# The context's modulation moved from the opening loop into the first eight projections

## The chip, the core and the metric

The kernel runs on one core of a Trainium2 chip. Its time is device time in microseconds (us); several runs of a kernel are summed up by their median. The core has five engines with a queue of instructions each: TensorE (PE, matrix products), VectorE (DVE), ScalarE (ACT), GpSimd (POOL) and SyncE (SP, which here only issues transfers). The transfers (DMA) between HBM and the core's memory are done by 16 DMA engines, whichever queue issues them. An instruction on a queue that waits holds up what stands behind it on the same queue.

## The reference, cut to what matters

One layer of a diffusion backbone works on a latent sequence `x` of 1024 tokens and on a context `ctx` of 256 tokens, both 1024 wide. Both are first modulated: scaled and shifted per channel, with vectors that a product of SiLU(c), or SiLU(c_ctx) for the context, with `w_ada` gives. The modulated tensors go through one wide input projection.

```
silu_c, silu_cc = silu(c), silu(c_ctx)
sh_m, sc_m, g_m, sh_f, sc_f, g_f = split(silu_c @ w_ada + b_ada, 6)
csh_m, csc_m, ...                = split(silu_cc @ w_ada + b_ada, 6)
h  = x   * (1 + sc_m)  + sh_m        # latent, 1024 x 1024
hc = ctx * (1 + csc_m) + csh_m       # context, 256 x 1024
gates, q, k, v, p_rwkv, p_sgu       = split(h  @ w_in)
_, _, k_c, v_c, p_rwkv_c, _         = split(hc @ w_in)   # what is used of them
```

Behind that come neighbourhood attention, an RWKV scan in both directions, a gated MLP over chunks (its input is `p_sgu`), the merging of the three, and a feed-forward part. The output is the latent stream alone. All is in float32.

## The kernel before, in words

Everything is laid out with channels on the 128 partitions, and a matrix of 1024 channels is 8 slices (k = 0 to 7). To keep the precision of float32 on PE, each factor is split into a high part (rounded to PE's format) and a low part (the rest), and a product is three matmuls: high x high, high x low, low x high (lines 306 to 308 in the opening loop, 220 to 222 in `mm` for the other projections). The high part is made by ACT, the low part by a subtraction on DVE or POOL.

`phase0a` is the first stage. It makes the modulated inputs and does 31 of the input projections, each of 128 output channels: a weight tile of 128 x 1024 is loaded by SP, split (ACT line 208; in this stage DVE line 212) and multiplied with the slices of the latent (two halves of 512 tokens, 48 matmuls) and, where the projection needs it, of the context (24 matmuls of 256 tokens).

The **opening loop** goes over k. For each k it

- loads two tiles of `w_ada`, 128 x 1024 each (scale and shift of the 128 channels of slice k), into a ring `w5` of 6 buffers;
- makes four rows, i.e. reductions along 1024 elements by DVE with `ada_row` (line 240): scale and shift for the latent (`cb[0]`, SiLU of c) and for the context (`cb[1]`). The latent's rows write their product to a tile `junk`, since the context's rows still need the weights. The results are columns of a small tile `mod`;
- loads the input slices `x` (128 x 1024) and `xc` (128 x 256), two buffers each;
- makes by ACT the high part `hh` (line 284) and, in place, the modulated `x` (line 285), and by POOL the low part `hl` (line 286); and likewise `ch` and `cl` for the context;
- for k below 4 loads and splits the weights of one of the projections 36 to 39 (`FIRST`; POOL line 237 makes the low part), which need the latent alone;
- adds slice k to the sums of the projections begun so far, which stay in eight banks of PSUM. The projection that begins at step k catches up on the slices before.

The opening's PE work is so 6, 18, 30, 42 and then four times 24 matmuls of 512 columns.

Behind the loop the low-rank weights of the decay are loaded and split (`lora_weights`, in a pool that takes the place of the opening's), then the constants of the gate, then the projections run in the order of the list `ms`: 36 to 39 (done already, only evacuated by ACT at line 444, shifted by DVE at lines 447 to 453, and stored from POOL's queue at line 455), 48 and 49 (inputs of the low-rank parts, with context), then for j = 0 to 3 the projections 40+j (RWKV k), 28+j (attention k), 44+j and 32+j, all with context, and among the first two j the four projections 55 to 58 of the gated MLP, which need the latent alone; last 51 to 54 and 50. Work that hangs on a projection (norms at lines 460 and 466, `lora`, transposes at 378 and 380) is put on a list `late` and issued up to three pieces per projection. From the seventh projection on, two more tiles of `w_ada` per projection are loaded into a ring `wa` of two buffers and reduced by DVE, 32 rows in all, for the later parts of the layer.

Who goes first on each engine isn't written by hand: a planner orders the instructions of each engine once, when the program is built, by the order in which the code names them and by its own reckoning of when their inputs are ready. So work can stand a little ahead of its place in the code.

Of the kernel before, what the change touches and what calls it, by code (L numbers as in the profile page):

```python
# [6 lines left out]
F32 = mybir.dt.float32  # L7
F32R = mybir.dt.float32r
BF16 = mybir.dt.bfloat16
AF = mybir.ActivationFunctionType  # L10
ALU = mybir.AluOpType
# [4 lines left out]
P = 128  # L16
D = 1024
S = 1024
CT = 256
# [12 lines left out]
FIRST = (36, 37, 38, 39)  # L32
LATE = 3
NWA, NW5, NT2 = 2, 6, 8
# [22 lines left out]
class Kern:  # L57
# [93 lines left out]
    def constants(self):  # L151
# [21 lines left out]
        self.ada = self.cp.tile([P, 48], F32, name="ada")  # L173

# [68 lines left out]
    def phase0a(self):  # L243
# [21 lines left out]
        for k in range(KT):  # L265
            x = self.bp.tile([P, S], F32, name="x", tag="x", bufs=2)
            xc = self.bp.tile([P, CT], F32, name="xc", tag="xc", bufs=2)
            m = self.cp.tile([P, 4], F32, name=f"mod{k}")
            w = [self.w5()[:, 0:D] for _ in range(2)]
            for i in range(2):  # L270
                nc.sync.dma_start(w[i], a["wada"][8 - 8 * i + k])
            for q in range(2):
                for i, b in enumerate((c["bsc"], bada)):
                    junk = w[i] if q else self.bp.tile([P, D], F32, name="junk", tag="junk", bufs=1)
                    self.ada_row(w[i], q, b[:, k:k + 1], m[:, 2 * i + q:2 * i + q + 1], junk)
            nc.sync.dma_start(x, a["xT"][k])
            nc.sync.dma_start(xc, a["cT"][k])
            hh = hp.tile([P, S], F32R, name=f"hh{k}")
            hl = hp.tile([P, S], F32R, name=f"hl{k}")
            ch = tp.tile([P, CT], F32R, name=f"ch{k}")  # L280
            cl = tp.tile([P, CT], F32R, name=f"cl{k}")
            for (xi, hi, lo, q, n) in ((x, hh, hl, 0, S), (xc, ch, cl, 1, CT)):
                sc_, sh_ = m[:, q:q + 1], m[:, 2 + q:3 + q]
                nc.scalar.activation(hi, xi, AF.Identity, scale=sc_, bias=sh_)
                nc.scalar.activation(xi, xi, AF.Identity, scale=sc_, bias=sh_)
                nc.gpsimd.tensor_tensor(lo, xi, hi.bitcast(F32), ALU.subtract)
            self.h.append((hh, hl))
            self.hc.append((ch, cl))
# [10 lines left out]
            for i, (z, (wh, wl, pss)) in enumerate(first.items()):  # L299
                for k2 in range(0 if i == k else k, k + 1):  # L300
                    q = slice(P * k2, P * k2 + P)
                    hh, hl = self.h[k2]
                    xs = (self.hc[k2], (hh[:, 0:512], hl[:, 0:512]), (hh[:, 512:S], hl[:, 512:S]))
                    for p, (xh, xl) in zip(pss, xs[3 - len(pss):]):
                        p = p[:, 0:xh.shape[1]]
                        nc.tensor.matmul(p, wh[:, q], xh, start=(k2 == 0), stop=False)
                        nc.tensor.matmul(p, wh[:, q], xl, start=False, stop=False)
                        nc.tensor.matmul(p, wl[:, q], xh, start=False, stop=(k2 == KT - 1))
        self.first = {z: w[2] for z, w in first.items()}
        self.cm_b.__exit__(None, None, None)  # L310
        self.cm_b, self.bp = self.pool("lora", side="right")
        self.lora_weights()
# [10 lines left out]
        ms = list(FIRST) + [48, 49]  # L323
        for j in range(4):
            ms += [40 + j, 28 + j] + [55 + 2 * j] * (j < 2) + [44 + j, 32 + j] + [56 + 2 * j] * (j < 2) + [51, 52] * (j == 3)
        ms += [53, 54, 50]
        na = 16
        self.late = []
        for i, m in enumerate(ms):
            late, self.late = self.late[:LATE], self.late[LATE:]  # L330
            (self.proj_gelu if m > 50 else self.proj_rwkv if m >= 36 else self.proj_kv)(m)
            self.run_late(late)
            for _ in range(2):
                if i >= 6 and na < 48:
# [5 lines left out]
        self.ada_rest()  # L340

# [1109 lines left out]
```

## Time and profile before

| | |
|---|---|
| median of 3 runs | 2454.48 us (2444.21 to 2455.71) |
| the profiled execution | 2457.49 us, its span 2455.7 us |
| opening loop's last matmul begins | 83.5 us |
| granted PE clock, mean | 0.973 |
| PE busy in the span | 2350.8 us of 2455.7 |
| HBM read and written | 248.85 MB and 85.99 MB, 136 GB/s over the span |

A line of a timeline shows the start, the duration, engine, source line and operation, then output `<-` inputs by the program's names, shapes, the count, and in brackets the idle time ahead of it and what ended that. A line of a group has the count, then busy time in us and the mean of one in ns, then the idle time ahead of its instructions. A line of the waits has the waiting engine, tile and line, whom it waited for, the sum in us, how many times and the longest. Matmuls overlap on PE, so the spacing of their starts is what counts, not the duration of one.

### The profile page before, as it was taken

How to read it: one execution, taken by the hardware profiler on the slowest of the kernel's cores; microseconds unless marked ns; L12 is line 12 of the kernel's file. 1: busy time of each engine (PE TensorE's matmuls, PEld its weight loads, DVE VectorE, ACT ScalarE, POOL GpSimd, SP SyncE). 2: the span in 40 equal slices, each digit the busy share in tenths (PEclk: the TensorE clock that was granted, in tenths of full speed). 3: DMA queues.
4: the chain of work that ended last, by engine and by line, in shares of the span. 5: the costliest groups of instructions: out<-in, count | busy, mean ns of one | idle time of the engine just before them, and what ended most of it. 6: DMA issues, size and time to landing. Idle time of an engine off the chain costs nothing.

```text
span 2455.7 us, 39343 instructions
## 1 busy us (share of the span) xinstructions
PE 2350.8 (96%) x14520; PEld 1850.5 (75%) x14520; DVE 1606.1 (65%) x3498; ACT 914.9 (37%) x1845; POOL 681.1 (28%) x714
## 2 busy tenths in 40 slices
PE   6999999999999999999999999999889999999997
PEld 4778888776777776677777778778678888887886
DVE  8884446347786778778358873778575555555835
ACT  4443334232343443344345552233433333333321
POOL 6221213441211111211121131142434333425402
PEclk9999999999897999999999999999889999999999
DMA  7675434553342343433277547655223222237551
GB/s 252 208 236 166 140 125 155 167 165 87 98 100 70 100 104 100 104 93 73 66 195 196 173 149 267 192 175 172 78 82 98 78 78 78 86 131 273 166 167 52
DMA packets 276116, 337.44 MB, mean 137 GB/s; under 512 B 123314, under 2 KB 194226, under 8 KB 275924
## 3 DMA queue, kind: packets, MB, share of 16 engines
q1 hardware_dynamic: 208804, 240.91, 33.1%
q10 hardware_dynamic: 54608, 51.40, 6.9%
q0 software_dynamic: 12512, 42.62, 4.7%
q8 instruction: 115, 1.88, 0.3%
q14 instruction: 77, 0.63, 0.1%
HBM read 248.85 MB, written 85.99 MB: 136 GB/s over the span
## 4 chain that ended last, share of the span: by engine, by line
PE 64%; DVE 8%; DMA 4%; issue 3%; ACT 2%; POOL 1%; SPq 0%; DVEq 0%; ACTq 0%; POOLq 0%
PE d L221 10%; PE d L222 10%; PE d L220 10%; PE d L1012 3%; PE pv L896 3%; PE d L1013 3%; PE d L1011 3%; PE ho L731 2%; PE gr L656 2%; PE sc L748 2%; PE pt L882 2%; PE sc L743 1%; PE sc L756 1%; PE gr L655 1%; PE sc L754 1%
## 5 line engine op out<-in xcount | busy, mean ns | idle before, releaser
L221 PE MATMUL d<-hl,wh 128*128 128x512 f32 x1056 | 435.8, 413 | 0.0
L222 PE MATMUL d<-hh,wl 128*128 128x512 f32 x1056 | 434.8, 412 | 0.0
L220 PE MATMUL d<-hh,wh 128*128 128x512 f32 x1056 | 433.8, 411 | 0.0
L221 PEld LDWEIGHTS d<-hl,wh 128*128 128x128 f32 x1056 | 202.1, 191 | 42.4 <-issue 0.7
L222 PEld LDWEIGHTS d<-hh,wl 128*128 128x128 f32 x1056 | 202.1, 191 | 42.3 <-issue 2.0
L220 PEld LDWEIGHTS d<-hh,wh 128*128 128x128 f32 x1056 | 201.9, 191 | 41.2 <-issue 1.6
L212 DVE TENSOR_TENSOR wl<-wr,wh 128x1024 fp32r<-128x1024 f32 x51 | 64.9, 1273 | 159.0 <-ACT wh L208 110.6
L208 ACT ACTIVATE wh<-wr 128x1024 fp32r<-128x1024 f32 x79 | 83.6, 1058 | 194.9 <-PE d L221 160.4
L212 POOL TENSOR_TENSOR wl<-wr,wh 128x256 fp32r<-128x256 f32 x112 | 85.6, 795 | 251.1 <-ACT wh L208 197.1
L237 DVE TENSOR_TENSOR o<-wr,o 128x1024 fp32r<-128x1024 f32 (+1 forms) x64 | 93.5, 1463 | 21.4 <-ACT o L234 21.0
L1012 PE MATMUL d<-dl,ah 128*128 128x512 f32 x252 | 98.7, 392 | 2.2 <-DVE dl L237 2.2
L768 ACT ACTIVATE rv<-sc,E 64x64 f32<-64x64 f32 x152 | 46.5, 308 | 143.2 <-DVE rv L767 131.9
L1011 PE MATMUL d<-dh,ah 128*128 128x512 f32 x252 | 98.8, 392 | 0.0
L1013 PE MATMUL d<-dh,al 128*128 128x512 f32 x252 | 98.7, 392 | 0.0
L234 ACT ACTIVATE o<-wr 128x1024 fp32r<-128x1024 f32 (+1 forms) x64 | 59.2, 926 | 104.0 <-PE d L221 73.1
L896 PE MATMUL pv<-pT,V 128*64 128x128 f32 (+2 forms) x640 | 92.1, 284 | 0.0
L237 DVE TENSOR_TENSOR al<-ar,ah 128x512 fp32r<-128x512 f32 x42 | 40.6, 981 | 78.3 <-ACT ah L234 78.3
L1006 POOL TENSOR_TENSOR wl<-wr,wh 128x1024 fp32r<-128x1024 f32 x16 | 42.6, 2661 | 169.0 <-ACT wh L1005 125.5
L734 DVE TENSOR_TENSOR X<-ho,Dt 48x192 f32<-48x192 f32 (+2 forms) x240 | 68.3, 285 | 24.3 <-PE ho L731 19.6
L1239 POOL TENSOR_TENSOR act<-act 128x512 f32<-128x512 f32 x22 | 28.8, 1309 | 193.9 <-issue 160.2
L896 PEld LDWEIGHTS pv<-pT,V 128*64 128x64 f32 (+2 forms) x640 | 69.1, 138 | 16.4 <-issue 10.8
L767 DVE TENSOR_SCALAR rv<-sc,E 64x64 f32<-64x64 f32 x152 | 41.8, 275 | 56.0 <-PE sc L756 38.9
(402 smaller groups left out, 6123.0 us busy)
## 6 DMA issues: line engine op xcount, KB each, us to landing
wr<-wgu SPq DMA_DIRECT2D x45, 512.0 KB
dr<-wdn SPq DMA_DIRECT2D x42, 512.0 KB
wa<-wada SPq DMA_DIRECT2D x32, 512.0 KB
wr<-win SPq DMA_DIRECT2D x31, 512.0 KB
wr<-win ACTq DMA_DIRECT2D x28, 512.0 KB
s_gt<-stg ACTq DMA_DIRECT2D x48, 256.0 KB
wr<-wbr SPq DMA_DIRECT2D x24, 512.0 KB
g<-s_gt SPq DMA_DIRECT2D x48, 256.0 KB
```

The source lines that it names most:

```text
L208: nc.scalar.activation(hi[:, :n], raw[:, :n], AF.Copy)
L212: (lo_eng or self.lo_eng).tensor_tensor(lo[:, q], raw[:, q], hi[:, q].bitcast(F32), ALU.subtract)
L220: nc.tensor.matmul(ps, w, xh, start=first and k == 0, stop=False)
L221: nc.tensor.matmul(ps, w, xl, start=False, stop=False)
L222: self.last = nc.tensor.matmul(ps, lo[:, P * k:P * k + P], xh, start=False, stop=last and k == n - 1)
L234: nc.scalar.activation(hi, src, AF.Copy)
L237: (lo_eng or nc.vector).tensor_tensor(lo, src, hi.bitcast(F32), ALU.subtract)
L734: nc.vector.tensor_tensor(X[z:z + n, :, t0:64], e[z:z + n], Dt[z:z + n, :, t0:64], ALU.add)
L896: nc.tensor.matmul(o, V[0:k, vt, 64 * e:64 * e + 64], pt[0:k, i, :], start=(i == 0), stop=(i == len(cols) - 1))
L1011: nc.tensor.matmul(ps, xh, wh, start=first, stop=False)
L1012: nc.tensor.matmul(ps, xh, wl, start=False, stop=False)
L1013: nc.tensor.matmul(ps, xl, wh, start=False, stop=last)
```

## The change

A new method `modulated(k, q)` makes slice k of the latent (q = 0) or of the context (q = 1). The opening loop calls it for the latent only: two rows on DVE instead of four, no `xc`, `ch` or `cl`; the rows write their products in place, without `junk`. The context's slice k is made behind projection number k of the list, for the first eight. Its two tiles of `w_ada` are loaded a second time, into the ring `wa` of two buffers. The order of the projections changes, so that the first eight need no context: 36 to 39, then 55 to 58, and then 48 and 49; the four aren't spread among the first two j any more. `lora_weights`, with the change of pools, comes behind the eighth projection. The 32 later rows begin at the tenth projection instead of the seventh.

```diff
         for k in range(KT):
-            x = self.bp.tile([P, S], F32, name="x", tag="x", bufs=2)
-            xc = self.bp.tile([P, CT], F32, name="xc", tag="xc", bufs=2)
-            m = self.cp.tile([P, 4], F32, name=f"mod{k}")
-            w = [self.w5()[:, 0:D] for _ in range(2)]
-            for i in range(2):
-                nc.sync.dma_start(w[i], a["wada"][8 - 8 * i + k])
-            for q in range(2):
-                for i, b in enumerate((c["bsc"], bada)):
-                    junk = w[i] if q else self.bp.tile([P, D], F32, name="junk", tag="junk", bufs=1)
-                    self.ada_row(w[i], q, b[:, k:k + 1], m[:, 2 * i + q:2 * i + q + 1], junk)
...
+            self.modulated(k, 0)
             if k < 4:
                 z = FIRST[k]
...
         self.first = {z: w[2] for z, w in first.items()}
-        self.cm_b.__exit__(None, None, None)
-        self.cm_b, self.bp = self.pool("lora", side="right")
-        self.lora_weights()
...
-        ms = list(FIRST) + [48, 49]
+        ms = list(FIRST) + [55, 56, 57, 58, 48, 49]
         for j in range(4):
-            ms += [40 + j, 28 + j] + [55 + 2 * j] * (j < 2) + [44 + j, 32 + j] + [56 + 2 * j] * (j < 2) + [51, 52] * (j == 3)
+            ms += [40 + j, 28 + j, 44 + j, 32 + j] + [51, 52] * (j == 3)
         ms += [53, 54, 50]
...
             self.run_late(late)
+            if i < 8:
+                self.modulated(i, 1)
+            if i == 7:
+                self.cm_b.__exit__(None, None, None)
+                self.cm_b, self.bp = self.pool("lora", side="right")
+                self.lora_weights()
             for _ in range(2):
-                if i >= 6 and na < 48:
+                if i >= 9 and na < 48:
...
+    def modulated(self, k, q):
+        nc, a, c, v = self.nc, self.a, self.c, self.v
+        n = (S, CT)[q]
+        x = self.bp.tile([P, n], F32, name=f"x{q}", tag=f"x{q}", bufs=2)
+        m = self.mod[:, 16 * q + 2 * k:16 * q + 2 * k + 2]
+        w = [self.tp.tile([P, D], F32, name="wa", tag="wa", bufs=NWA) if q else self.w5()[:, 0:D] for _ in range(2)]
+        for i, b in enumerate((c["bsc"], v("bada"))):
+            nc.sync.dma_start(w[i], a["wada"][8 - 8 * i + k])
+            self.ada_row(w[i], q, b[:, k:k + 1], m[:, i:i + 1], w[i])
+        nc.sync.dma_start(x, a["cT" if q else "xT"][k])
+        p = self.tp if q else self.hp
+        hi, lo = (p.tile([P, n], F32R, name=f"h{z}{q}_{k}") for z in "hl")
+        nc.scalar.activation(hi, x, AF.Identity, scale=m[:, 0:1], bias=m[:, 1:2])
+        nc.scalar.activation(x, x, AF.Identity, scale=m[:, 0:1], bias=m[:, 1:2])
+        nc.gpsimd.tensor_tensor(lo, x, hi.bitcast(F32), ALU.subtract)
+        (self.hc if q else self.h).append((hi, lo))
```

More of the change, by code (lines that the diff above doesn't have):

```diff
@@ L173, in constants @@
         self.ada = self.cp.tile([P, 48], F32, name="ada")
+        self.mod = self.cp.tile([P, 32], F32, name="mod")
     def scratch(self):
@@ L265, in phase0a @@
         for k in range(KT):
-            x = self.bp.tile([P, S], F32, name="x", tag="x", bufs=2)
-            xc = self.bp.tile([P, CT], F32, name="xc", tag="xc", bufs=2)
-            m = self.cp.tile([P, 4], F32, name=f"mod{k}")
-            w = [self.w5()[:, 0:D] for _ in range(2)]
-            for i in range(2):
-                nc.sync.dma_start(w[i], a["wada"][8 - 8 * i + k])
-            for q in range(2):
-                for i, b in enumerate((c["bsc"], bada)):
-                    junk = w[i] if q else self.bp.tile([P, D], F32, name="junk", tag="junk", bufs=1)
-                    self.ada_row(w[i], q, b[:, k:k + 1], m[:, 2 * i + q:2 * i + q + 1], junk)
[L276 to L288, printed above, removed]
+            self.modulated(k, 0)
             if k < 4:
@@ L302, in phase0a @@
                     hh, hl = self.h[k2]
-                    xs = (self.hc[k2], (hh[:, 0:512], hl[:, 0:512]), (hh[:, 512:S], hl[:, 512:S]))
-                    for p, (xh, xl) in zip(pss, xs[3 - len(pss):]):
-                        p = p[:, 0:xh.shape[1]]
+                    xs = ((hh[:, 0:512], hl[:, 0:512]), (hh[:, 512:S], hl[:, 512:S]))
+                    for p, (xh, xl) in zip(pss, xs):
                         nc.tensor.matmul(p, wh[:, q], xh, start=(k2 == 0), stop=False)
```

## The prediction, on record before the run

> **What bounds the kernel now.** I read the page of the profile first: TensorE (PE) is busy nearly the whole span, so a change gains only where PE stands still, or where what it works on could be there sooner.
>
> ```profile
> span 2455.7 us, 39343 instructions
> ...
> PE 2350.8 (96%) x14520; PEld 1850.5 (75%) x14520; DVE 1606.1 (65%) x3498; ACT 914.9 (37%) x1845; POOL 681.1 (28%) x714
> ```
>
> The change touches the projection stage, so the second view is the busy time by stretches there (columns: busy time and count of PE, PEld, DVE, ACT, POOL, then granted clock, DMA share, GB/s).
>
> ```profile
> 15.00:36.00 21.00, 12.17 (x28) 7.28 (x28) 20.82 (x19) 9.30 (x11) 17.29 (x7) 1.00 0.69 243
> 36.00:84.00 48.00, 40.62 (x167) 31.84 (x168) 41.77 (x42) 23.37 (x28) 29.10 (x15) 0.96 0.68 227
> 84.00:140.00 56.00, 54.29 (x279) 45.04 (x279) 52.87 (x67) 18.32 (x25) 3.76 (x7) 1.00 0.65 189
> 140.00:160.00 20.00, 15.66 (x59) 11.75 (x58) 9.69 (x13) 9.63 (x13) 0.00 (x0) 0.83 0.74 228
> 160.00:300.00 140.00, 139.90 (x708) 116.83 (x707) 81.87 (x109) 48.89 (x81) 38.76 (x51) 1.00 0.57 177
> ```
>
> PE idles in the opening loop (up to 84 us), a little around 140 to 160, and hardly anywhere else: 139.90 of 140 us behind that. Third, the waits of PE up to 520 us, which name who ended those gaps:
>
> ```profile
> PE d L307 <- POOL hl L286: 11.0, 7, 3.6
> ...
> PE gr L466 <- DVE w L460: 4.3, 1, 4.3
> ...
> PE d L222 <- DVE wl L212: 1.7, 1, 1.7
> ```
>
> In the opening PE waits for POOL's low halves, `hl`. Why POOL is late shows in the groups of instructions of the first 84 us, and in the timelines of DVE and POOL over one step k:
>
> ```profile
> L286 POOL TENSOR_TENSOR hl<-x,hh 128x1024 fp32r<-128x1024 f32 x8 | 22.2, 2771 | 28.4 <-ACT x L285 28.4
> L240 DVE CUSTOM_DVE_ANT_0 w<-w,cb,der 128x1024 f32<-128x1024 f32 x8 | 20.2, 2528 | 0.2
> L240 DVE CUSTOM_DVE_ANT_0 junk<-w,cb,c_pv 128x1024 f32<-128x1024 f32 x8 | 20.1, 2506 | 0.0
> ...
> L240 DVE CUSTOM_DVE_ANT_0 w<-w,cb,c_pv 128x1024 f32<-128x1024 f32 x8 | 13.3, 1666 | 0.2
> L286 POOL TENSOR_TENSOR cl<-xc,ch 128x256 fp32r<-128x256 f32 x8 | 12.8, 1599 | 0.0
> L240 DVE CUSTOM_DVE_ANT_0 junk<-w,cb,der 128x1024 f32<-128x1024 f32 x8 | 12.7, 1592 | 5.2 <-DMA w<-wada 5.2
> ...
> L237 POOL TENSOR_TENSOR w<-wr,w 128x1024 fp32r<-128x1024 f32 x2 | 6.7, 3370 | 0.0
> L237 POOL TENSOR_TENSOR wl<-wr,wh 128x1024 fp32r<-128x1024 f32 x2 | 6.7, 3337 | 0.0
> ```
> ```profile
> 8.25 1.28 DVE L240 CUSTOM_DVE_ANT_0 junk<-w,cb,der 128x1024 f32<-128x1024 f32 x1 [4.85 <-DMA w<-wada]
> ...
> 42.30 1.28 DVE L240 CUSTOM_DVE_ANT_0 junk<-w,cb,der 128x1024 f32<-128x1024 f32 x1
> 43.51 0.08 DVE L240 DVE_READ_ACCUMULATOR2_ANT mod<- 128x1 f32 x1
> 43.63 3.28 DVE L240 CUSTOM_DVE_ANT_0 w<-w,cb,der 128x1024 f32<-128x1024 f32 x1
> 46.84 0.08 DVE L240 DVE_READ_ACCUMULATOR2_ANT mod<- 128x1 f32 x1
> 46.84 3.41 DVE L240 CUSTOM_DVE_ANT_0 junk<-w,cb,c_pv 128x1024 f32<-128x1024 f32 x1
> ```
> ```profile
> 43.40 2.43 POOL L286 TENSOR_TENSOR hl<-x,hh 128x1024 fp32r<-128x1024 f32 x1 [2.10 <-ACT x L285]
> 45.78 3.38 POOL L237 TENSOR_TENSOR w<-wr,w 128x1024 fp32r<-128x1024 f32 x1
> 49.13 1.72 POOL L286 TENSOR_TENSOR cl<-xc,ch 128x256 fp32r<-128x256 f32 x1
> ...
> 78.22 0.75 POOL L286 TENSOR_TENSOR cl<-xc,ch 128x256 fp32r<-128x256 f32 x1
> ```
>
> The same DVE row takes 1.28 us at 42.30 and 3.28 us at 43.63, while POOL's `hl` runs. The times fit one rule: the two take turns. POOL starts when DVE's row ends (43.58) and holds until 45.78, 2.2 us; the DVE row that was issued at 43.63 then needs 1.1 us and ends at 46.91; POOL's next, issued at 45.78, ends at 49.16, 2.25 us after that. So the price of a DVE row is 1.21 us (42.30 to 43.51), of a wide POOL subtraction 2.25 us and of a narrow one about 0.6 us. The sum over the opening: 32 rows x 1.21 = 38.7, 12 wide subtractions (8 `hl`, 4 weight halves) x 2.25 = 27.0, 8 narrow ones x 0.6 = 4.8, together 70.5 us. From the first row at 8.25 that is 78.8 us; the last POOL instruction ends at 78.97. The opening is bound by DVE and POOL in turn, to within 0.2 us, not by DMA (227 to 243 GB/s) and not by PE.
>
> **The opening after the change.** Half of the rows (16) and all 8 narrow subtractions leave. Left are 16 x 1.21 + 27.0 = 46.4 us of turns, which from 8.25 could be done at 54.7 us. Now PE's own work decides.
>
> ```profile
> 64.27 0.80 PE L307 MATMUL d<-hl,wh 128*128 128x512 f32 x1 [3.07 <-POOL hl L286]
> 64.86 0.63 PE L308 MATMUL d<-hh,wl 128*128 128x512 f32 x1
> 65.28 0.63 PE L306 MATMUL d<-hh,wh 128*128 128x512 f32 x1
> ...
> 66.99 0.48 PE L307 MATMUL d<-hl,wh 128*128 128x512 f32 x1
> ...
> 70.96 0.39 PE L306 MATMUL d<-hh,wh 128*128 128x512 f32 x1
> ...
> 76.42 0.40 PE L306 MATMUL d<-hh,wh 128*128 128x512 f32 x1
> ...
> 83.70 0.28 PE L220 MATMUL d<-ch,wh 128*128 128x256 f32 x1
> ```
>
> From 70.96 to 76.42 PE does the 24 matmuls of one step: 0.2275 us each. The opening has 6, 18, 30, 42 and four times 24 of them, 192 in all. Once `hl` of step 2 is there, 168 are left at most, 38.2 us. When is it there? By turns: seven rows (8.5) and five wide subtractions (11.2) from 8.25 give 28.0; two microseconds more for ACT, which makes `hh` and scales `x` between a row and its subtraction, give 30. PE ends at 30 + 38.2 = 68.2, say 68.5, against 83.7: 15.2 us gained. Steps 3 to 7 do not hold it: their turns are over by about 58 us, behind which only the last 24 matmuls (5.5 us) must follow. Bounds: 66 us, were ACT hidden, and 74.5 us, if step 2 comes no earlier than now:
>
> ```profile
> 32.92 3.36 POOL L286 TENSOR_TENSOR hl<-x,hh 128x1024 fp32r<-128x1024 f32 x1
> ```
>
> (36.3 + 38.2). So the gain lies between 9.2 and 17.7 us. SyncE's queue runs in order, and `x` of step k waits there for `hl` of step k-2 with the next weights behind it; in my count this holds a row back by at most the microseconds already allowed.
>
> **The moved work.** The eight `wada` pairs are read a second time (16 x 512 KB), 16 rows go to DVE, 16 narrow passes to ACT, where they stand among the evacuations, and the 8 narrow subtractions to POOL, whose queue also issues the stores of `r` (line 455) and so may make them wait for a shift. They have the time until projection 48, the first that uses context. Ahead of it PE has the four projections 55 to 58, which are moved forward: 4 x 48 x 0.2275 = 43.7 us, so it comes to 48 at about 68.5 + 43.7 + 2 = 114 us. The rows go through a ring of two buffers; what such a row costs then is shown by the later ones of the same ring:
>
> ```profile
> L240 DVE CUSTOM_DVE_ANT_0 wa<-wa,cb,c_pv 128x1024 f32<-128x1024 f32 x20 | 25.5, 1281 | 11.8 <-DMA wa<-wada 11.7
> ```
>
> These 20 lie between 97.0 and 164.5 us: 3.4 us each, with the waits for their loads. The new ones can begin when the opening's last loads are issued, about 53 us by the count above. 53 + 16 x 3.4 + 3 for ACT and POOL = 110 us: in time with 4 us to spare. I set this at nothing. The cover is PE's 43.7 us on the four latent projections; where it ends, each 0.1 us more per row costs PE 1.6 us (the rival below). It can't bring a gain, since 48 has nothing to do earlier. The low-rank weights, now read behind the rows, are needed only after 49: hidden too. The stage's loads and stores between 53 and 114 us, by their sizes (8.4 MB for `wada`, 3.1 MB for six weights, 1 MB each for context and low-rank weights, 0.8 MB for the gate's constants, 3.1 MB stored), are 17.4 MB, an estimated 285 GB/s, against 189 and 228 in the stretches shown.
>
> **The hand-over at the loop's end.** Here is a new wait. DVE makes the low weight half of the next projection, and works in order:
>
> ```profile
> 80.42 0.75 DVE L447 TENSOR_SCALAR w<-w,der 128x1024 f32<-128x1024 f32 x1 [5.88 <-ACT w L444]
> ...
> 85.46 1.22 DVE L212 TENSOR_TENSOR wl<-wr,wh 128x1024 fp32r<-128x1024 f32 x1
> ...
> 86.73 0.38 PE L222 MATMUL d<-ch,wl 128*128 128x256 f32 x1 [1.71 <-DVE wl L212]
> ```
>
> Five shift instructions stand ahead of it (80.42 to 85.46), and PE waits 1.71 us. After the change, context rows are also queued there; one to three of them, 1.2 to 3.6 us, come on top, and without the context's matmuls PE has less to do meanwhile. Everything on PE is queued behind that matmul, and ACT's evacuations and the shifts of the next projections behind PE. I take 2 us more (0 to 5). The gap at 64.27 shows that a stop of 3.07 us also costs the clock: up to 66.99 the matmuls go at 0.43 us, seven of them 0.2 us late each, 1.4 us. The Trainium skill (page TensorE: Matmul & The Clock Gate, section Why this matters for your kernels) warns of idle gaps over about 3 us between bursts of matmuls; the trace agrees, and by that rule a hand-over of 3.7 us would make the sum 1.4 us worse.
>
> **The gap at 147.** The wait of 4.3 us for L460 (a granted clock of 0.83 in that stretch) costs, with the slow restart priced at 64.27, 5.7 us. L460 stands on DVE among the rows of the other shifts and gates, which begin at the tenth projection now instead of the seventh; but the projection that needs L460, 40, comes at the eleventh instead of the seventh. I keep it at no change (between 5.7 gained and a second such gap, 5.7 lost). The rest of the stage has the same matmuls; with 55 to 58 no longer spread between projections whose DVE work is heavy, DVE has fewer pauses, for which I bound 0 to 3 us and take 0.
>
> **Sum.** -15.2 + 2 = -13.2 us. The profiled execution took 2457.49 us with a span of 2455.7, 3 us above the median of the runs; 2457.5 - 13.2 = 2444.3 there, and 2454.5 - 13.2 = 2441.3 against the median. PE is on the path almost without a break behind the stage, so what is gained here is kept.
>
> **Rivals.** *The gap at 147 goes too*: 13.2 + 5.7 = 18.9, giving 2435.6. For it: it hangs on one row and its load. Against: rows and loads are as dense as before. *DVE's queue eats the gain*: hand-over at its worst (5), the pauses (3) and another late weight half, some 10 us in all, giving about 2451. For it: between 53 and 114 us DVE gets 16 rows (16 x 1.28 = 20), twelve shift instructions (5.04 us for five, so 12), and seven halves of weights (7 x 1.22 = 9), 41 of 61 us, in an order fixed beforehand. Against: between 84 and 140 us it is busy for 52.87 of 56, and PE for 54.29, the 1.71 of the hand-over being all that is missing. *The opening is held by loads*: SyncE's order, with each step's `x` behind an `hl` and the weights behind `x`, brings step 2 no sooner than now: 9.2 - 2 = 7 us gained, 2447. Against: the `hl` that `x` waits for come sooner themselves. *Slower*: the ring of two buffers becomes the bound. Rows may take (114 - 53 - 3) / 16 = 3.6 us each; each 0.1 above costs 1.6 us at the start of 48. At 4.4 us the gain is gone, at one and a half times today's 3.4, 5.1 us, PE loses 24 us and the kernel takes 2465. For it: the 285 GB/s, and that rows that wait hold the weight halves behind them. Against: idle DVE before 66 us lets the first rows run at once. That the context isn't moved at all can't be: the loop simply no longer makes it.
>
> **Chances.** Forecast (9 to 17 gained) 0.50; the gap goes too 0.14; DVE's queue 0.17; loads 0.07; slower 0.12. A measurement of this kernel tells about 0.5%, 12.3 us, from no change. The forecast lies on that line: 0.30 of its 0.50 is above. Faster: 0.30 + 0.14 = 0.44. Slower by over 0.5%: 0.09 of the last case. Same: 0.47. The range goes from 2433 (the gap gone and 2 us more) to 2454 (nothing gained); some 0.12 lies above it and 0.05 below. The likeliest case's own range is 2437 to 2446.
>
> **What would show it.** Right: 16 rows and no `cl` ahead of about 55 us; `hl` waits of PE down from 11 us to under 5, all in the first 30 us; first matmul of projection 55 near 68.5; 192 matmuls without a gap from step 2; the context's rows at L240 over by 110. Wrong: the first matmul of 55 after 75; a wait of PE for a `ch` or `cl` at 48; waits for `wl` of 56 to 58; a PE wait for L460 longer than 4.3.

## The result, and the profile after

The changed kernel takes 2472.14 us in the median of 6 runs (2463.14 to 2477.46), beside 2455.1 for the kernel before on the same chip: a ratio of 1.0074, with a 95% interval of 1.0044 to 1.0103. It is slower by 0.7%, and it lies above the range that was forecast (2433 to 2454). The profiled execution has a span of 2472.1 us, 16.4 more than before.

The page, whose first lines answer to those of before:

```profile
span 2472.1 us, 39365 instructions
...
PE 2358.0 (95%) x14520; PEld 1846.0 (75%) x14520; DVE 1603.1 (65%) x3498; ACT 909.8 (37%) x1840; POOL 677.1 (27%) x714
```

PE has as many instructions as before and is busy 7.2 us longer. That is the first sign that not only waits came in.

The opening went as forecast. The groups of instructions of its first 69 us, and PE around its end (lines have moved: DVE's rows are now in L241, `hl` in L337, the projections' three matmuls in L221 to L223, `wl` in L213):

```profile
L337 POOL TENSOR_TENSOR hl<-x,hh 128x1024 fp32r<-128x1024 f32 (+1 forms) x9 | 23.6, 2619 | 24.1 <-ACT x L336 24.1
L241 DVE CUSTOM_DVE_ANT_0 w<-w,cb,c_pv 128x1024 f32<-128x1024 f32 x8 | 22.9, 2859 | 0.0
L241 DVE CUSTOM_DVE_ANT_0 w<-w,cb,der 128x1024 f32<-128x1024 f32 x8 | 17.6, 2196 | 11.2 <-DMA w<-wada 11.2
```
```profile
68.99 0.39 PE L286 MATMUL gr<-hh,w 128*128 128x512 f32 x1
69.21 0.40 PE L221 MATMUL d<-hh,wh 128*128 128x512 f32 x1
```

Sixteen rows on DVE instead of 32, and the next projection's first matmul at 69.21 instead of 83.70: 14.5 us gained, where 15.2 were forecast. The stretches and the waits of PE behind it:

```profile
36.00:69.00 33.00, 33.00 (x145) 26.87 (x145) 23.35 (x21) 14.18 (x15) 15.83 (x7) 1.00 0.74 249
69.00:90.00 21.00, 14.88 (x62) 10.56 (x60) 21.00 (x28) 9.93 (x15) 4.48 (x6) 0.91 0.72 243
90.00:101.00 11.00, 8.81 (x30) 7.02 (x31) 7.24 (x11) 2.40 (x4) 1.75 (x3) 0.71 0.91 312
101.00:155.00 54.00, 54.00 (x273) 44.95 (x272) 25.19 (x36) 17.53 (x28) 4.75 (x6) 1.00 0.89 238
155.00:195.00 40.00, 30.27 (x146) 25.35 (x145) 36.52 (x60) 11.89 (x14) 8.43 (x12) 0.91 0.62 216
195.00:260.00 65.00, 56.39 (x277) 45.98 (x276) 51.33 (x76) 22.35 (x35) 24.23 (x30) 0.95 0.75 237
260.00:400.00 140.00, 139.83 (x725) 116.46 (x725) 78.31 (x90) 51.17 (x85) 34.83 (x50) 1.00 0.40 133
```
```profile
PE d L223 <- DVE wl L213: 18.0, 3, 8.7
PE gr L376 <- ACT t L378: 6.0, 1, 6.0
...
PE d L285 <- POOL hl L337: 1.7, 1, 1.7
```

PE is unbroken from 36 to 69 us, and the wait for `hl` fell from 11.0 to 1.7. Then come three holes, in 69 to 90, 155 to 195 and 195 to 260. In the first DVE is busy for 21.00 of 21 us while PE waits for DVE's `wl`; in each, the granted clock also falls.

The second loss is in no view of waits. The gate-up part of the feed-forward, which the change doesn't touch, by the first and last start of 22 products on POOL in it, first before, then after:

```profile
L1239 POOL TENSOR_TENSOR act<-act x22: 1288/1300/1599, 1801.2 to 2193.9; 128x512 f32<-128x512 f32 x22
```
```profile
L1237 POOL TENSOR_TENSOR act<-act x22: 1275/1287/1594, 1811.0 to 2211.4; 128x512 f32<-128x512 f32 x22
```
And a stretch of 100 us inside it, again before and after:

```profile
1885.00:1985.00 100.00, 100.00 (x438) 82.05 (x438) 57.14 (x71) 31.43 (x41) 36.50 (x25) 1.00 0.25 79
```
```profile
1895.00:1995.00 100.00, 100.00 (x431) 80.56 (x430) 54.83 (x67) 30.87 (x40) 36.32 (x25) 1.00 0.24 79
```

1801.2 to 2193.9 us is 392.7 us, 1811.0 to 2211.4 is 400.4. PE is 100% busy in both, at a granted clock of 1.00, but does 431 matmuls in 100 us instead of 438. The mean time between the starts of two neighbouring matmuls there is 233.3 ns instead of 228.9.

The spans in parts (us), with four of the experiments below. The columns are the kernel before, the changed one, before with 128 bytes less, before with the new order alone, the same with the rows held, before with 64 bytes more, and the best version (gate-up is counted here from another product of the same part, 1.7 us shorter in both):

| part | before | after | e2 | e5 | e13 | e16 | e14 |
|---|---|---|---|---|---|---|---|
| opening | 83.7 | 69.2 | 84.3 | 83.8 | 84.3 | 83.8 | 68.4 |
| projections, up to the first RWKV matmul | 431.5 | 457.2 | 435.0 | 447.2 | 440.3 | 425.7 | 438.8 |
| from there to gate-up | 1292.2 | 1290.7 | 1291.1 | 1298.0 | 1277.8 | 1286.6 | 1287.7 |
| gate-up | 391.0 | 398.7 | 398.7 | 391.0 | 391.0 | 387.2 | 387.2 |
| rest | 257.3 | 256.3 | 257.4 | 257.4 | 256.7 | 256.2 | 257.2 |
| span | 2455.7 | 2472.1 | 2466.5 | 2477.4 | 2450.1 | 2439.5 | 2439.3 |

So the change gained 14.5 in the opening and lost 25.7 in the projections and 7.7 in gate-up (-1.5 and -1.0 in the two others). The third row is code that no edit touches. In the table it moves by some 20 us, and over all runs further, with the clock that was granted in it: 1270.7 us at 0.98 in e15, 1309.7 at 0.95 in e11. A straight line through all timed runs, one offset per kernel, gives 2.04 us for 0.001 of mean clock. Where "at the same clock" stands below, that line was used. It takes some of a kernel's own stops out too, since the clock falls around a stop (0.71 in the stretch from 90 to 101 us above), so the plain ratio stands first.

### The profile page after: what moved, and what is told of

Same layout as the page of the kernel before. It is cut to its first block, busy times and chain, and to the rows that moved or that the text cites. A ratio compares the mean times of both kernels' runs of the same rounds, so it can differ in the third digit from the quotient of the medians.

```text
span 2472.1 us, 39365 instructions
## 1 busy us (share of the span) xinstructions
PE 2358.0 (95%) x14520; PEld 1846.0 (75%) x14520; DVE 1603.1 (65%) x3498; ACT 909.8 (37%) x1840; POOL 677.1 (27%) x714
## 4 chain that ended last, share of the span: by engine, by line
PE 80%; DVE 10%; issue 4%; POOL 2%; DMA 2%; ACT 2%; SPq 0%; DVEq 0%; POOLq 0%; ACTq 0%
PE d L222 15%; PE d L223 15%; PE d L221 15%; PE pv L894 3%; PE d L1010 3%; PE d L1011 3%; PE d L1009 3%; PE ho L729 2%; PE gr L654 2%; PE sc L746 2%; PE sc L741 1%; PE gr L653 1%; PE pt L880 1%; PE sc L754 1%; PE sc L752 1%
## 5 line engine op out<-in xcount | busy, mean ns | idle before, releaser
L223 PE MATMUL d<-hh,wl 128*128 128x512 f32 (+1 forms) x1200 | 480.7, 401 | 18.0 <-DVE wl L213 18.0
L221 PE MATMUL d<-hh,wh 128*128 128x512 f32 (+1 forms) x1200 | 478.7, 399 | 3.9 <-ACT w L442 1.4
L222 PE MATMUL d<-hl,wh 128*128 128x512 f32 (+1 forms) x1200 | 479.3, 399 | 0.0
L223 PEld LDWEIGHTS d<-hh,wl 128*128 128x128 f32 x1200 | 230.9, 192 | 65.3 <-DVE wl L213 18.9
L221 PEld LDWEIGHTS d<-hh,wh 128*128 128x128 f32 x1200 | 230.3, 192 | 50.8 <-issue 3.0
L222 PEld LDWEIGHTS d<-hl,wh 128*128 128x128 f32 x1200 | 230.6, 192 | 44.3 <-issue 0.2
L213 DVE TENSOR_TENSOR wl<-wr,wh 128x1024 fp32r<-128x1024 f32 x51 | 65.5, 1284 | 143.9 <-ACT wh L209 122.9
L213 POOL TENSOR_TENSOR wl<-wr,wh 128x256 fp32r<-128x256 f32 x112 | 84.6, 786 | 249.5 <-ACT wh L209 201.7
L894 PEld LDWEIGHTS pv<-pT,V 128*64 128x64 f32 (+2 forms) x640 | 68.4, 137 | 16.3 <-issue 10.7
```

What stands on the lines that cost most here:

```text
L213: (lo_eng or self.lo_eng).tensor_tensor(lo[:, q], raw[:, q], hi[:, q].bitcast(F32), ALU.subtract)
L221: nc.tensor.matmul(ps, w, xh, start=first and k == 0, stop=False)
L222: nc.tensor.matmul(ps, w, xl, start=False, stop=False)
L223: self.last = nc.tensor.matmul(ps, lo[:, P * k:P * k + P], xh, start=False, stop=last and k == n - 1)
L894: nc.tensor.matmul(o, V[0:k, vt, 64 * e:64 * e + 64], pt[0:k, i, :], start=(i == 0), stop=(i == len(cols) - 1))
```

## The experiments

**e1 and e2: the memory addresses.** The change puts one tile of 128 bytes per partition in place of eight of 32. Everything allocated behind it on that side, the weights among it, moves down by 128 bytes; the tiles they are multiplied with, on the other side, don't. e1 gives the changed kernel its 256 bytes back; e2 takes 128 from the kernel before and does nothing else.

```diff
-        self.mod = self.cp.tile([P, 32], F32, name="mod")
+        self.mod = self.cp.tile([P, 64], F32, name="mod")        # e1, in the changed kernel
```
```diff
+        self.mod = self.cp.tile([P, 32], F32, name="mod")        # e2, in the kernel before
-            m = self.cp.tile([P, 4], F32, name=f"mod{k}")
+            m = self.mod[:, 4 * k:4 * k + 4]
```

> The changed kernel, with the tile mod twice as wide (256 bytes per partition instead of 128), so that all tiles behind it stand where they stood before the change. Theory: the 128 bytes by which the change shifted the weights cost 4.4 ns per matmul in the gate-up stage; its matmuls go back from 233.3 to about 229 ns and the kernel is 6 to 8 us faster than the changed one, about 2465. Rival: the slower matmuls belong to that run, not to the addresses; then nothing changes beyond what two runs differ by, and this kernel stays at 2472.

> The kernel before, with its eight small mod tiles (256 bytes in all) put into one of 128 bytes: nothing else differs, all tiles behind it move down by 128 bytes. Theory of the addresses: gate-up's matmuls at 233 ns instead of 229, the kernel 6 to 8 us slower than before, about 2462. Rival: the same time as before, 2455.

The stretch of gate-up that was shown above, in e1 and in e2:

```profile
1885.00:1985.00 100.00, 100.00 (x438) 82.06 (x437) 55.71 (x67) 32.32 (x42) 37.80 (x26) 1.00 0.25 79
```
```profile
1895.00:1995.00 100.00, 100.00 (x431) 80.12 (x430) 54.69 (x67) 31.89 (x41) 36.61 (x26) 1.00 0.24 79
```

e1: 2451.13 us, ratio to before 1.0018 (0.9991 to 1.0046), spacing in gate-up 228.9 ns again; its stops stay (8.89 us at 92.00, 8.69 at 185.09, 6.35 at 249.43), and its projections take 459.9 us, no less than the 457.2 of the changed kernel. e2: 2458.58 us, 1.0035 (1.0007 to 1.0064), spacing 233.3, and its span is 10.8 us longer, 7.7 of them in gate-up and 3.5 in the projections. At the same clock it is 9.5 us (7.3 to 11.7) over before, of the changed kernel's 12.3. By the plain ratios it is 0.35% of 0.74%. So some half to three quarters of the measured slowdown is a side effect of the allocation.

**e8, e12, e16: other addresses.** The kernel before with a wider constant tile: 128 bytes more (e8), 64 more (e12, a single execution; e16, the same kernel timed).

```diff
-        self.ada = self.cp.tile([P, 48], F32, name="ada")
+        self.ada = self.cp.tile([P, 80], F32, name="ada")        # e8; 64 columns in e12 and e16
```

> The kernel before with 128 bytes more in a constant tile, so that the weights lie 128 bytes higher instead of 128 lower. If what counts is the weights' offset in steps of 256 bytes against the tiles of the other side, the gate-up goes at 233.3 ns a matmul as with 128 bytes less, and the time is 7 to 11 us over before. If it is a matter of which side of a 512-byte line they lie on, or of how much memory is free, the gate-up stays at 228.9 ns or takes a third value.

> The kernel before with 64 bytes more in a constant tile. Only the matmuls' spacing in the gate-up is read: if it goes by the offset in steps of 256 bytes with one good place, some value between 228.9 and 233.3 ns or above; if only the 128-byte line counts, 228.9 (the same as before) or 233.3.

> The kernel before with 64 bytes more in a constant tile and nothing else, timed. If the address is worth what the spacing in the gate-up shows, 387.2 in place of 391.0 us, and some in the projections, whose stage ended 5.5 us earlier in the look: 4 to 9 us under before, a ratio of 0.996 to 0.998. If the look was luck (a granted clock or the projections' stops), under 4 us.

e8: 2464.92 us, 1.0050 (1.0024 to 1.0077), spacing 233.3. e12: 2448.36 us. e16: 2441.36 us, 0.9959 (0.9939 to 0.9979). The same stretch of gate-up, in e8 and in e16:

```profile
1895.00:1995.00 100.00, 100.00 (x430) 80.56 (x430) 55.40 (x67) 31.62 (x42) 37.70 (x26) 1.00 0.24 79
```
```profile
1885.00:1985.00 100.00, 100.00 (x443) 82.80 (x442) 55.21 (x68) 32.70 (x44) 39.99 (x28) 1.00 0.26 85
```

With 64 bytes more every matmul is 226.7 ns behind the last. So the kernel before wasn't at its best place either: -128, 0, +64 and +128 bytes give 233.3, 228.9, 226.7 and 233.3 ns. In the projections the starts of neighbouring 128x512 matmuls (100 to 500 us) move too: 231.7 ns before, 233.3 in the changed kernel and 227.4 in e16, whose projections are 5.8 us shorter. The equal ends fit a rule that repeats every 256 bytes; 128 or 64 bytes can't be the period, since steps of that size change the spacing. Whether it does repeat, and which accesses make the difference, these runs don't tell. The Trainium skill (page SBUF — State Buffer, section Operand start alignment) asks of a float32 operand only that it start at a multiple of 4 bytes, which is a rule of what is allowed and not of speed. All four places meet it, and the measured times differ.

**e3: the store of sums.** `ada_rest` stores a small tile of 1024 values (`s_gm`) across its own order (`rearrange("m p -> p m")`). The store is issued at 143.2 us in the changed kernel:

```profile
L914 POOL DMA_DIRECT2D s_gm<-der x1: 939/939/939, 143.2 to 143.2; - x1
...
DMA to landing us min/median/max: 11.3/11.3/11.3
```
```profile
q1 hardware_dynamic: 48, 0.14, 58.0%
```

It needs 11.3 us for 4 KB, and meanwhile (150 to 155 us, the second fence) the queue of loads moves 0.14 MB though its packets hold the DMA engines for 58% of the time. A row on DVE waits for its load then, and a chain follows, first on DVE, then on ACT:

```profile
156.58 1.28 DVE L241 CUSTOM_DVE_ANT_0 wa<-wa,cb,c_pv 128x1024 f32<-128x1024 f32 x1 [8.64 <-DMA wa<-wada]
...
164.12 1.28 DVE L241 CUSTOM_DVE_ANT_0 wa<-wa,cb,c_pv 128x1024 f32<-128x1024 f32 x1
...
180.79 1.22 DVE L213 TENSOR_TENSOR wl<-wr,wh 128x1024 fp32r<-128x1024 f32 x1
```
```profile
164.23 1.27 ACT L476 ACTIVATE w<-w 128x1280 f32<-128x1280 f32 x1 [17.25 <-DVE w L451]
...
168.75 1.06 ACT L209 ACTIVATE wh<-wr 128x1024 fp32r<-128x1024 f32 x1
```

DVE is held for 8.64 us and so comes late to the shift of projection 48. ACT stands for 17.25 us until that shift is done, with the `wh` of 28 behind it. DVE makes the `wl` of 28 only at 180.79, behind gate norms and shifts, and PE stops for 8.67 us until 182.06. e3 issues the store and the sums ahead of it behind a later shift; PE's order is the same.

```diff
-            nc.vector.scalar_tensor_tensor(sh[:, b0:b1 - 1], raw[:, b0 + 1:b1], mn, sh[:, b0:b1 - 1], ALU.mult, ALU.add)
+            self.shift[m] = nc.vector.scalar_tensor_tensor(sh[:, b0:b1 - 1], raw[:, b0 + 1:b1], mn, sh[:, b0:b1 - 1], ALU.mult, ALU.add)
...
-        self.ada_rest()
+        with self.tc.issue_after(self.shift[42].ins): self.ada_rest()
```

> The changed kernel, with the store of the gate row s_gm (4 KB in pieces of 4 bytes) and the few DVE instructions ahead of it held back until projection 42; order on PE and of all other instructions is the same. Theory: this store blocks the transfers for some 10 us, a row on DVE waits 8.6 us for its load because of it, and through DVE and ACT PE loses 8.7 us at 182 us and about 1 at 159. Without it that row waits under 3 us, the stop of 8.7 us is gone or under 2, and the kernel is 8 to 11 us faster than the changed one, about 2462. Rival: it is the second reading of wada that fills the queues; then the row still waits 6 us or more, and the time stays within 3 us of 2472.

2467.37 us, 1.0068 (1.0042 to 1.0094). What DVE's rows wait for, 100 to 200 us, in the changed kernel and in e3 (the sum, the count, the longest):

```profile
DVE wa L241 <- DMA wa<-wada: 32.7, 16, 8.6
```
```profile
DVE wa L241 <- DMA wa<-wada: 24.0, 15, 4.8
```

And the queue of loads from 150 to 155 us, without the store:

```profile
q1 hardware_dynamic: 327, 1.18, 76.9%
```

It moves 1.18 MB there instead of 0.14. The longest wait falls from 8.6 to 4.8 us, PE's stop from 8.67 (at 182) to 3.79 (at 176); the projections take 453.3 us instead of 457.2. The store is worth 3.9 of the 25.7, where 8 to 11 were expected. The Trainium skill (page DMA: Bandwidth & Descriptors, section Specifications) puts the smallest transfer at full rate at 512 bytes; the 11.3 us agree in direction, though that one such store holds up the loads of another queue is what these two traces show.

**e4: the first stop.** DVE in the changed kernel from the first projection's `wl` to the second's, and what PE does (some rows left out):

```profile
66.20 1.23 DVE L213 TENSOR_TENSOR wl<-wr,wh 128x1024 fp32r<-128x1024 f32 x1 [4.55 <-ACT wh L209]
67.34 0.75 DVE L445 TENSOR_SCALAR w<-w,der 128x1024 f32<-128x1024 f32 x1
68.01 1.28 DVE L241 CUSTOM_DVE_ANT_0 wa<-wa,cb,der 128x1024 f32<-128x1024 f32 x1
...
86.72 1.27 DVE L241 CUSTOM_DVE_ANT_0 wa<-wa,cb,c_pv 128x1024 f32<-128x1024 f32 x1
...
89.19 1.28 DVE L241 CUSTOM_DVE_ANT_0 wa<-wa,cb,der 128x1024 f32<-128x1024 f32 x1
...
90.40 1.74 DVE L213 TENSOR_TENSOR wl<-wr,wh 128x1024 fp32r<-128x1024 f32 x1
```
```profile
92.19 0.79 PE L223 MATMUL d<-hh,wl 128*128 128x512 f32 x1 [8.31 <-DVE wl L213]
92.78 0.63 PE L221 MATMUL d<-hh,wh 128*128 128x512 f32 x1
...
96.19 0.49 PE L223 MATMUL d<-hh,wl 128*128 128x512 f32 x1
```

Between the two `wl` stand the shifts of 36 to 39 and seven of the context's rows, without a pause; the seven rows take 9.8 us. PE is done with projection 55 and with a few matmuls of 56 that need no `wl`. It stops for 8.31 us and then goes on at 0.43 us a matmul until 96.19. e4 lets POOL make the low halves of 55 to 58:

```diff
-        hi, lo = self.load_w(self.a["win"][m], 1024)
+        hi, lo = self.load_w(self.a["win"][m], 1024, self.nc.gpsimd if 55 <= m <= 58 else None)
```

> The changed kernel, with the low weight halves of projections 55 to 58 made by POOL instead of DVE. Theory: PE's stop of 8.3 us at 84 to 92 us is DVE's order alone (seven context rows and twelve shifts ahead of a weight half whose inputs were there at 70); POOL is free, so the stop is gone, 8 to 10 us with its slow restart, and the first context projection starts as much earlier, unless the context's rows are then what it waits for. About 2463. Rival: the loads of the ring are the limit; then PE waits as long at 57, 58 or 48, and the time stays within 3 us of 2472.

2457.65 us, 1.0049 (1.0021 to 1.0077). The stop at 92 is gone, the projections take 448.4 us, 8.8 less; 5.6 us of waiting for 28's `wl` remain, at 171. So what the context's rows cost here, they cost by their place ahead of `wl` on DVE.

**e5: the order alone.** The kernel before, its context made in the opening as it was, with the new list `ms` and the later rows from the tenth projection.

> The kernel before with nothing of the change but its order of projections (55 to 58 ahead of 48, 49 and 28, 32) and the later rows from the tenth projection; context is made in the opening loop as before, and the weights' addresses are those of before. My theory (the stops of TensorE come from the context's rows on VectorE ahead of wl, the gate-up from the 128 bytes): the order alone costs little, time within 4 us of the kernel before at the same granted clock, the gate-up at 228.9 ns a matmul, no stop of over 4 us between 84 and 150. Rival (the order itself is the cost: the gate norms' store and the later rows now stand beside 28): 5 to 10 us slower than before, with a stop of 6 to 9 us ahead of 28's second half, at about 15 us later than in the changed kernel.

2480.63 us, 1.0123 (1.0076 to 1.0170); 13.0 us over before at the same clock. My theory fell: the order alone, which the prediction had at no cost, makes the projections 15.7 us longer (447.2 against 431.5). PE's waits from 84 to 300 us (those for `wl` are at the hand-over and ahead of 40 and 28, at 168 and 186):

```profile
PE d L222 <- DVE wl L212: 8.1, 3, 3.5
PE gr L466 <- issue: 7.0, 1, 7.0
PE d L220 <- ACT t L428: 3.3, 1, 3.3
```

The gap at 147 is gone here, and these stops took its place. 457.2 less 447.2 leaves 10.0 us of the changed kernel's projections for the rest, if the costs simply add, which no run shows. The stop of 8.31 us with nine matmuls 0.2 us late each, 1.8, would fill it, and e4 measured 8.8. But the slower matmuls at the changed addresses lie in it too: 1448 of 128x512 at 1.6 ns each (233.3 less 231.7) are an estimated 2 us. So the context's rows are worth some 8 to 10 us, and the account is not exact to better than that.

**e6 and e7: the mends together.** e6 is the changed kernel with the edits of e1, e3 and e4; in e7 the later rows also are named from the fourteenth projection on (`if i >= 13` for `if i >= 9`).

> The changed kernel with the three mends at once: 128 bytes more in the row tile (weights at the addresses of before), the rest of the rows' sums and their store issued behind the shift of projection 42, and the lower halves of 55 to 58 made on GpSimd. My theory (the costs are separate): -10 to -11 of the layout, -4 of the store, -5 of the halves, together 19 us under the changed kernel and 4 to 6 us under the kernel before, a ratio to before of about 0.998. Rival (the ordering only moves its stops about): stops of 5 to 9 us come back elsewhere in the projections, and the time is at or above the kernel before.

> As the kernel with three mends, and the later rows begin at the fourteenth projection in place of the tenth. My theory (the stop ahead of 28's second half comes from VectorE held by rows that wait for their loads): that stop falls from some 5 us to under 2, and the time is 2 to 5 us under the kernel with three mends. Rival (the stop is 28's own place beside the gate norms): the stop stays, and the time is the same within 2 us.

e6: 2455.35 us, 0.9998 (0.9970 to 1.0027). e7: 2448.75 us, 0.9998 (0.9973 to 1.0024). Both the same as before; at the same clock 2.5 and 4.0 us under it (each 2 either way). The changed kernel lost 12.3 by that measure, so the mends are worth about 15 together, less than the 19 expected; the stop ahead of 28's half stays in both, 6.02 and 6.01 us at 173 and 170. But e7 is no test of the rows: on DVE they start in the same order as in e6 and up to 3 us earlier (the first at 121, 124 and 129 us there, at 119, 121 and 126 here). The planner had pulled them ahead.

**e9 and e10: why the order costs.** e9 is e5 with rows from the fourteenth projection; e10 has besides 55, 56, 57 and 50 in front, and 58 with its gate norms back where it was. The edit of e10 against e9:

```diff
-        ms = list(FIRST) + [55, 56, 57, 58, 48, 49]
+        ms = list(FIRST) + [55, 56, 57, 50, 48, 49]              # e10
...
-            ms += [40 + j, 28 + j, 44 + j, 32 + j] + [51, 52] * (j == 3)
-        ms += [53, 54, 50]
+            ms += [40 + j, 28 + j, 44 + j, 32 + j] + [58] * (j == 1) + [51, 52] * (j == 3)
+        ms += [53, 54]
```

> The kernel before with only the new order of projections, as in the run that came 12.8 us over before at the same granted clock, but with the later rows from the fourteenth projection in place of the tenth. Theory A (the order costs because the rows, each waiting for its load on VectorE, now stand among 48, 49 and the gate norms): most of it goes, 2 to 6 us over before, and the stops of 2.6 and 3.5 us ahead of wl at 168 and 186 are gone. Theory B (the order costs by the gate norms and the evacuations of 48 and 49 next to each other): 9 to 13 us over before still, with the stops at the same places.

> The kernel before with the order 55, 56, 57, 50 ahead of 48 and 49, with 58 (and the gate norms behind it) back where the kernel before has it, and the later rows from the fourteenth projection. Theory A (rows): the same as the run with rows later alone, within 3 us. Theory B (gate norms beside 48 and 49): 4 to 8 us under that run, within 3 us of the kernel before.

e9: 2472.32 us, 1.0082 (1.0061 to 1.0102), projections 447.7 us. But it is no test either: the rows start on DVE at the same times as in e5 (99, 103, 104 and so on to 224 us, within 2.1 us of one another), since the planner had pulled them ahead again. e10: 2479.75 us, 1.0107 (1.0071 to 1.0143). Its projections are shorter (435.8 us, and 441.3 with the some 5.5 us of 26 matmuls that come later in it, against 447.7), but there is still a stop of 8.53 us at 206, and from 500 to 900 us the granted clock is 0.90, against 0.92 before and 0.94 in e5; the part up to gate-up takes 1308.5. So the norms' place explains 6 of the 16 us at most.

**e11: all of it, with e10's order.**

> The changed kernel with the four mends (128 bytes more, the sums' store behind the shift of 42, lower halves of 55 to 58 on GpSimd, rows from the fourteenth projection) and the order with 50 in place of 58, 58 and its norms back where they were. Theory A: the same as the four mends with the changed order, 3 to 4 us under before at the same granted clock. Theory B (norms): the stop of 6.0 us at 170 goes, 8 to 12 us under before, a ratio of about 0.996.

2467.19 us, 1.0066 (1.0043 to 1.0089). A miss: the stop at 170 went and one of 6.43 us at 183 came; from 500 to 900 us the clock is 0.90 again, and the mean clock of its runs, 0.966, the lowest of all. At the same clock it would be 4.5 us under before (2.1 to 6.9), so the two measures disagree here. What in this order lowers the clock there stays open.

**e13 and e14: the rows held.** All later rows with their loads behind the shift of projection 40. This time the order on DVE does change: none of them stands among 55 to 58, 48 and 49. e13 is e5 with that; e14 the changed kernel with the three mends (the tile so wide that the weights lie 64 bytes above their place in the kernel before) and the rows held; e15 is e7 at that address.

```diff
-                if i >= 9 and na < 48:
-                    w = tp.tile([P, D], F32, name="wa", tag="wa", bufs=NWA)
+                if i >= 11 and na < 48:
+                    with self.tc.issue_after(self.shift[40].ins):
+                        w = tp.tile([P, D], F32, name="wa", tag="wa", bufs=NWA)
...
+        self.mod = self.cp.tile([P, 80], F32, name="mod")        # e14 and e15
```

> The kernel before with only the new order of projections, and all the later rows (loads and sums) issued behind the shift of projection 40, so that VectorE has none of them among 55 to 58, 48 and 49. Theory A (the order costs because rows that wait for their loads hold VectorE ahead of wl and of the evacuations of 48 and 49): the 447.2 us from the opening's end to the first RWKV matmul fall to 431 to 437, and the stops ahead of wl at 168 and 186 and ahead of the norm's matmul at 208 go or fall under 2 us each. Theory B (the gate norms and the shifts of 48 and 49 on VectorE, rows or not): 443 to 448, the stop of 7 us ahead of the norm's matmul stays. A third way (the rows run into the chains of k and v later): the early stops go and others of the same sum come after 230.

> The changed kernel with the three mends (the sums' store behind the shift of 42, lower halves of 55 to 58 on GpSimd, and the row tile widened, here so far that the weights lie 64 bytes above their place in the kernel before), and the later rows held behind the shift of 40. Theory A (rows): the opening's end at 69, the projections 431 to 437 us after it, the gate-up at 226.7 ns a matmul: 18 to 24 us under the kernel before, a ratio of about 0.992. Theory B: as the next run, within 3 us.

> The kernel with three mends whose rows begin at the fourteenth projection, with the weights 64 bytes above their place in the kernel before. The address and the mends are separate: 4 us under the kernel before for the mends (at the same granted clock) and 4 to 9 more for the address (the gate-up at 226.7 in place of 228.9 ns is 3.8 us of it), a ratio of 0.995 to 0.997.

e13: 2459.89 us, 1.0046 (1.0015 to 1.0078). PE's waits from 84 to 520 us:

```profile
PE gr L379 <- ACT t L381: 7.6, 2, 5.7
PE gr L467 <- DVE ada L911: 5.0, 1, 5.0
PE d L222 <- DVE wl L212: 1.9, 1, 1.9
```

(The last is the hand-over.) The stops at 168, 186 and 208 are gone, so the rows that stood there did make them; 5.7, 5.0 and 1.9 us came at 237, 270 and 312. It is the third way of the three expected: the projections fall from 447.2 to 440.3 only. e14: 2438.28 us, 0.9941 (0.9921 to 0.9961), with the lowest median; its projections take 438.8 us, where 431 to 437 were expected. e15: 2442.93 us, 0.9965 (0.9942 to 0.9987). Both are faster than the two kernels, and so is e16.

**e17 and e18: projections put back.** e17 is e13 with 57 and 58 behind 28 and 29, where the kernel before has 55 and 57; e18 is e14 with 58 behind 28 and the context's last two slices behind 57.

```diff
-        ms = list(FIRST) + [55, 56, 57, 58, 48, 49]
+        ms = list(FIRST) + [55, 56, 48, 49]                      # e17
...
-            ms += [40 + j, 28 + j, 44 + j, 32 + j] + [51, 52] * (j == 3)
+            ms += [40 + j, 28 + j] + [57 + j] * (j < 2) + [44 + j, 32 + j] + [51, 52] * (j == 3)
```

> The kernel before with 55 and 56 alone ahead of 48 and 49, 57 and 58 between the projections of k and v again (behind 28 and 29), and the later rows held behind the shift of 40. Theory (the rest of the order's cost is that 55 to 58 no longer stand between the projections of k and v, whose chains on ACT, VectorE and the ring of small tiles they covered): the projections take 431 to 436 us from the opening's end to the first RWKV matmul, and the stops after 230 fall from 12.6 us to under 6 in all. Rival (the held rows alone make those stops, the order has no part left): 438 to 443, with the same sum of stops.

> The version with mends, rows held and the weights 64 bytes higher, with 58 put back behind 28 and the context's last two slices made behind projection 57. If the cover counts and the context is there in time for 48 (it has 11 us less): 2 to 6 us under that version, about 2433. If the context is late: TensorE stops for ch or cl at 48, some 5 us or more, and the time is the same or above, 2438 to 2444.

e17: 2460.75 us, 1.0044 (1.0013 to 1.0076), projections 440.1 us, with these waits:

```profile
PE gr L467 <- DVE w L461: 7.3, 1, 7.3
PE gr L379 <- DVE w L454: 4.8, 2, 4.1
PE d L222 <- DVE wl L212: 2.0, 1, 2.0
```

The rival came true: the same sum of stops with half of the cover back. e18: 2438.56 us, 0.9942 (0.9912 to 0.9971), no different from e14; 4.1 us of waits for the context's halves came in, as its second branch had it.

## Why the prediction was wrong

- **The opening** (-15.2): right, in its mechanism too. Measured -14.5. The latent's last row on DVE ended at 54.2 us and its last `hl` at 59.4 (the count by turns had given 55 and 58), and PE, unbroken from 36 us on, bounded the loop once half the rows had left.
- **The moved work, "I set this at nothing"**: wrong, and not by the rival that was kept for it. The context was there in time: its sixteen rows ran from 57.7 to 112.1 us, 3.4 us each as forecast, and PE never waited for it. But what hides a row's time does not hide its place: seven rows stood on DVE ahead of a `wl` that PE needed 8.31 us sooner. The cover that the prediction named, PE's 43.7 us on four projections, itself needs DVE for each weight half. Cost some 8 to 10 us (8.8 in e4; the remainder over e5 is 10.0, with an estimated 2 of addresses in it). The outcome, slower, had 0.12 in the chances, but for a ring of two buffers that becomes the bound, and that did not happen.
- **The hand-over** (+2): the place was wrong. The `wl` of 55 was made at 66.20, ahead of the rows, and cost nothing; the price came one projection later, at 56, where the prediction lists "waits for `wl` of 56 to 58" only as a sign of failure.
- **"The gap at 147 ... no change", "0 to 3 us and take 0"** for the order: wrong, 15.7 (e5). The gap itself went (the changed kernel's PE waits 0.2 us for the same matmul), as the first rival had it, but its 5.7 us were not gained. Stops at 159, 182, 219, 223 and 246 us came in, 18.2 us in all. About 7 of the 15.7 are the later rows that wait for their loads among 48 and 49 (e13). The rest is not settled: held rows bring stops of their own, and putting two projections back doesn't shorten them (e17). The store of sums is 3.9 (e3, in the changed kernel); in the kernel before it was issued at 130.7 and landed 10.2 us later, just ahead of the gap at 147. A row on DVE waits 5.50 us for its load until 144.76 there; that the store is the cause in that kernel too was not tested.
- **"The rest of the stage has the same matmuls", "what is gained here is kept"**: the count is the same, but not the time of one. The smaller constant tile costs 9.5 us at the same clock (0.35% by the plain ratio) and 10.8 in the profiled execution, 7.7 of it in gate-up, 1700 us behind the change (e2). No part of the working looked at addresses.
- **The sum**: forecast -13.2. By the profiled executions: opening -14.5, order +15.7, context's rows with the slower matmuls beside them +10.0, gate-up +7.7, and -2.5 in the rest: +16.4. The 10.0 is a remainder, and each figure is one execution's. Once mended, the idea is worth a little: e14 and the kernel before at the same address (e16) take 2438.28 and 2441.36 us, 6.5 apart at the same clock (3.7 to 9.2), while their plain intervals overlap. Not all of that need be the idea's: e14 also issues the store later and holds the rows, and the kernel before wasn't run with these two. At 68.4 us for the opening it gains the forecast 15, and the projections (438.8 against 425.7) give 13 back.

## What to carry to other kernels

A change that adds, removes or merges a small tile moves everything allocated behind it: compare the matmuls per 100 us in a stage that the change doesn't touch, before explaining the total by the change's idea, and try a few paddings (here 64 bytes made the kernel before 0.4% faster). When work is moved into the shadow of an engine, price its place on its own engine's queue ahead of what the shadow itself needs, not only its duration. A planner may put moved code back: see the order on the engine before reading the time.

## What the runs showed of the hardware

- The spacing of back-to-back 128x512 matmuls in gate-up, at a granted clock of 1.00, depends on where the tiles of the weights' side lie: 226.7 ns (+64 bytes, e16), 228.9 (0), 233.3 (-128 in e2 and +128 in e8).
- A 4 KB store across the order of its tile took 11.3 us to land and held up the loads of another queue meanwhile: 0.14 MB in 5 us on the queue of loads, and 1.18 MB in the same 5 us when the store came later (e3).
- After a stop of 8.31 us PE's matmuls started 0.43 us apart for nine matmuls, then 0.23.
